# When the second layer's adaLN vectors are made, how many tiles of the halved half-steps stay plain, and the sizes of the feed-forward pieces

## The chip, the core and the metric

The kernel runs on one core of a Trainium2 chip. The metric is the device time of one execution in microseconds. Before the change it is 2717.73 us, the median of three runs (2717.67 to 2719.18). The engines are TensorE (PE in the rows, PEld its weight loads), VectorE (DVE), ScalarE (ACT), GpSimd (POOL) and SyncE (SP); the last two only issue transfers here.

## What is computed

A diffusion trunk of two layers over 512 latent and 256 context tokens of width 1024, in fp32. Both streams use the same weights; the adaLN vectors (shift, scale and gate) differ. Per layer:

```python
x += 1/2 * gate1 * SwiGLU_a(mod1(RMSNorm(x)))   # first half-step, d_ff = 2816
h  = mod2(RMSNorm(x)); p = h @ W_in             # mixer: pool | retention q,k,v,g | conv
x += gate2 * concat[pool, retention, conv] @ W_out
x += 1/2 * gate3 * SwiGLU_b(mod3(RMSNorm(x)))   # second half-step
# mod(h) = h * (1 + scale) + shift;  SwiGLU(h) = (silu(h @ w1) * (h @ w3)) @ w2
# 9 vectors per layer and stream: silu(c) @ w_mod;   at the end RMSNorm of the latent stream
```

## The kernel before

Every fp32 product is three matmuls of the faster fp32r type (lines 164 to 166): each operand is split into a high part (a cast, ScalarE, line 159) and a low part (a subtraction, VectorE, line 160). So every weight block (128x1024, `raw`, then `wh` and `wl`) costs ScalarE and VectorE about a microsecond each, and every product's result does too. Weights are loaded by SyncE in the order of `weight_order`; four split blocks stand ready at most.

The stages follow one another: half-step (0,0) by `ffn`, mixer 0, half-step (0,1) by `ffn_halved`, half-step (1,0) by `ffn_halved`, mixer 1, half-step (1,1) by `ffn`, which has only the latent stream left, in two halves. A half-step has 22 tiles of 128 hidden channels. `ffn` takes them in pieces (PIECES): for every tile the products `up` of w1 and w3 for the context (256 columns) and the latents (512 columns), then `silu` and the product `g`, and after the piece the products `down` into 8 output tiles, added to x. In the last piece the context's `down` come first, then the latents'; each group's squares are summed (`acc`), and `norm_steps` makes the next norm: `ms` (a matmul that sums the squares), a chain of small VectorE operations, `diag`, `rstd` (a matmul that spreads the result), then `ht` and `h`.

`ffn_halved` works in pairs of tiles. It saves matmuls with a scheme of seven products instead of eight (`up_halved`: 7 products of 4 k-tiles, 3 matmuls of 384 columns each, for two weight halves and two column halves of h). This needs sums and differences of the weights (VectorE, lines 601 to 609) and of h: `differences` makes four sets, one per k-tile, each of 8 VectorE operations, 3 casts on ScalarE and 3 subtractions on VectorE. The first pair of tiles is plain, as in `ffn`, and the differences are made meanwhile. x is not in SBUF in these stages: `add_kept` scales a `down` result on ScalarE (`xpart`, line 229), and a transfer from GpSimd's queue adds it to `xkept` in HBM (line 231); only the last pair loads x again.

The adaLN vectors of a layer are nine chunks (l, j). A chunk (`mod_chunks`) is 8 loads of 512 KB (`wm`, two buffers, SyncE's queue), 32 multiply-additions on VectorE (`macc`, lines 319 and 321), 4 turns and 4 folds (`mturn`, `mrow`, lines 329 and 330), one matmul `mods` (line 337) and 8 additions (line 346). It is a generator that runs as a task beside the main program: `spawn(task, delay)` lets it begin after so many microseconds of TensorE work planned so far, each `yield` names the wait to its next step, `poll` runs what is due, and `drain` runs all that is left at once. A scheduler then sets the order of each engine from dependences and the order in which the program was written. Before the change the chunks (0,3) to (0,8) and (1,0) to (1,2) run beside (0,0), (1,3) and (1,4) beside (0,1), (1,5) to (1,8) beside (1,0). Chunk (0,2) is a task of its own, drained after the `up` products of the first piece of (0,0).

Of the kernel before, what the change touches and what calls it, by code (L numbers as in the profile page):

```python
# [15 lines left out]
P = 128  # L16
# [4 lines left out]
DEPTH = 2  # L21
DFF = 2816
NF = DFF // P
PIECES = (4, 4, 4, 4, 4, 2)
MAXP = max(PIECES)
HEADS = 4
WINDOWS = (2, 4, 8, 16)
# [8 lines left out]
NFIRST = 2  # L36
# [1 line left out]


HALVED = ((0, 1), (1, 0))  # L40
HK, HN, SUB = KD // 2, NT // 2, 2
PARKED = ((0, 1), (1, 1), (0, 2), (1, 0))


# [37 lines left out]
class Kernel:  # L82
# [436 lines left out]
    def weight_order(self):  # L519

        ins = self.ins

        def halved(l, s):
            f0 = 0
            for npc in PIECES:
                w2 = ins["w2"][l, s, :, f0 * D : (f0 + npc) * D].rearrange("p (d f n) -> p d f n", d=KD, f=npc)
                for a in range(0, npc, SUB):
                    for f in range(f0 + a, f0 + a + SUB):
                        both = [ins["w13"][l, s, f, :, m * 1024 : (m + 1) * 1024] for m in range(2)]
                        if f < NFIRST:  # L530
                            yield from both
                        else:
                            yield both
                    for d in range(0, KD, 4):
                        yield w2[:, d : d + 4, a : a + SUB]
                f0 += npc

        def ffn(l, s):
            f0 = 0
            for npc in PIECES:  # L540
                for f in range(f0, f0 + npc):
                    for m in range(2):
                        yield ins["w13"][l, s, f, :, m * 1024 : (m + 1) * 1024]
                n = npc * P * per_block(npc)
                for c in range(f0 * D, (f0 + npc) * D, n):
                    yield ins["w2"][l, s, :, c : c + n]
                f0 += npc

        for l in range(DEPTH):
            yield from (halved if (l, 0) in HALVED else ffn)(l, 0)  # L550
            for i in range(4, 8) if l < DEPTH - 1 else range(4):
                yield ins["w_feat"][l, i]
            for i in range(4) if l < DEPTH - 1 else range(4, 8):
                yield ins["w_feat"][l, i]
            for i in range(4):
                yield ins["w_tok"][l, i]
            for i in (10, 11, 12, 13, 8, 9, 14, 15, 16, 17):
                yield ins["w_feat"][l, i]
            for i in range(2):
                for dt2 in range(KD // 2):  # L560
                    yield ins["w_out"][l, i, dt2]
            yield from (halved if (l, 1) in HALVED else ffn)(l, 1)

    def fetch(self, src):
        raws = []
        for a in src if isinstance(src, list) else [src]:
            n = a.shape[-1] if len(a.shape) == 2 else 1024
            raws.append(self.raw(n))
            to = raws[-1] if len(a.shape) == 2 else raws[-1].rearrange("p (d f n) -> p d f n", d=4, f=SUB)
            self.nc.sync.dma_start(to, a)  # L570
        return raws

# [145 lines left out]
    def differences(self, h, T):  # L718

        nc = self.nc  # L720
        for kt in range(HK):
            b11, b12, b21, b22 = self.sums(h, kt)
            nc.vector.tensor_sub(b11, b12, b11)
            nc.vector.tensor_sub(b12, b22, b12)
            nc.vector.tensor_sub(b22, b22, b11)
            nc.vector.tensor_sub(b21, b21, b22)
            for i, t in ((3, b12), (2, b22), (4, b21)):
                for p in range(2):
                    T[i][p][kt] = self.slot("t", F32R)[:, :HN]
                self.split(t, T[i][0][kt], T[i][1][kt])  # L730
            yield 3.6

    def first_difference(self, h):
        nc = self.nc
# [64 lines left out]
    def ffn_halved(self, l, s, h, starts, grps, ends, done):  # L799
# [1 line left out]
        idx = 2 * s  # L801
        accs = {}
        T = {i: [[None] * HK for _ in range(2)] for i in (2, 3, 4)}
        for f0 in range(0, NF, SUB):
            g = self.empty()
            last = f0 == NF - SUB

            def load():
                for st in (CTX, LAT):
                    self.load_x(st, self.kept[st])  # L810

            if f0 == 0:
                ws = {f: self.w13() for f in range(SUB)}
                for grp in starts:
                    self.need(grp)
                    if grp is starts[-1]:
                        task = self.spawn(self.differences(h, T), 1.0)
                    self.up(ws, range(SUB), h, g, grp)
                self.drain(task)
                self.first_difference(h)  # L820
            else:
                for f in range(SUB):
                    self.up_halved(f, h, T, g, load if last and f == SUB - 1 else None)
            w2 = []

            def down(dt, grp, ps, fs):
                self.products([(ps, w2[dt // 4], dt % 4 * SUB * P + fs[0] * P)], g, grp, fs, fs[0] == 0, fs[-1] == SUB - 1)

            if last:
                w2 = [self.weights() for _ in range(2)]  # L830
                for grp in ends:
                    for dt in range(KD):
                        ps = self.psum("down")[:, : grp[2]]
                        down(dt, grp, ps, range(SUB))
                        xd = self.xs(dt, grp)
                        nc.vector.scalar_tensor_tensor(xd, ps, self.gate(l, idx, grp[0], dt), xd, op0=ALU.mult, op1=ALU.add)  # L836
                        self.square(dt, grp, accs)
                    done(grp, accs)
            else:
                for d in range(0, KD, 2):  # L840
                    if d % 4 == 0:
                        w2.append(self.weights())
                    these = [(dt, grp, self.psum("down")[:, : grp[2]]) for dt in (d, d + 1) for grp in grps]
                    for fs in ((0,), (1,)):
                        for dt, grp, ps in these:
                            down(dt, grp, ps, fs)
                    for dt, grp, ps in these:
                        self.add_kept(dt, grp, ps, self.gate(l, idx, grp[0], dt))


    def project(self, w, h, grp, s):
# [444 lines left out]
    def run(self):  # L1296
# [59 lines left out]
            self.up(w0, [1], h, g, G_CTX)  # L1356

        self.first = [self.spawn(self.mod_chunks([(0, 2)], 4.0), 10.0)]
        later = self.spawn(self.mod_chunks([(0, j) for j in range(3, 9)] + [(1, j) for j in range(3)], 6.0), 80.0)
        for l in range(DEPTH):  # L1360
            last = l == DEPTH - 1
            grps = (G_LAT,) if last else both
# [9 lines left out]
                self.drain(later)  # L1372
                self.decays()
            else:
                later = self.spawn(self.mod_chunks([(l, j) for j in range(5, 9)], 11.2), 20.0)
                self.ffn_halved(l, 0, h, both, both, both, done)
                self.drain(later)

# [1 line left out]
            self.mixer(l, h1, grps, cuts, done)  # L1380

            if not last:
                later = self.spawn(self.mod_chunks([(l + 1, j) for j in range(3, 5)], 6.84), 40.0)
                h, done = next_norm(l + 1, 0)
            else:
                done = self.final
# [136 lines left out]
```

## Time and profile before

| | before |
|---|---|
| median of 3 runs | 2717.73 us |
| the profiled execution | 2717.79 us, its span 2715.9 us |
| TensorE busy | 2533.0 us, 93% |
| VectorE, ScalarE, GpSimd busy | 68%, 39%, 11% |
| granted TensorE clock, mean | 0.966 |

The profile comes from one execution. Its span runs from the first to the last instruction; 1.9 us of the time lie around it. A busy TensorE is not one at its peak, since matmuls are pipelined; so the distance from one matmul's start to the next, the share of its weight loads and the granted clock are read beside the busy time. In a row of a timeline the brackets at the end hold the time in which the engine stood idle just before, and what ended it.

### The profile page before, as it was taken

What the parts mean: (1) busy time and instruction counts of PE and PEld (TensorE: products, weight loads), DVE (VectorE), ACT (ScalarE), POOL (GpSimd) and SP (SyncE); (2) the same over time, 40 slices, a digit from 0 to 9 for tenths busy, and PEclk for the clock granted to TensorE, in tenths of its full rate; (3) what the DMA queues carried; (4) which work ended last, traced back from release to release, by engine and by line L of the source; (5) the groups of instructions that cost most, each with busy time, mean ns of one, the idle gap of its engine ahead of it and who ended that gap; (6) DMA issues with size and microseconds to landing.
All of it is one profiled execution on the core that took longest, in us unless ns stands there. A gap on an engine that the chain in (4) does not pass through costs nothing.

```text
span 2715.9 us, 36761 instructions
## 1 busy us (share of the span) xinstructions
PE 2533.0 (93%) x13906; PEld 2247.8 (83%) x13906; DVE 1835.3 (68%) x3430; ACT 1050.3 (39%) x1840; POOL 304.4 (11%) x348
## 2 busy tenths in 40 slices
PE   8999999980999997999999869999998999999997
PEld 4888888870888887899999759999998888888886
DVE  6957767779597688775454787776776696643434
ACT  3221221221134544545555445555554245422222
POOL 0000000000000202323323022424240001000000
PEclk9999999995999998999999989999999999999998
DMA  7533433342132535775757446878675234322221
GB/s 260 166 106 124 143 129 124 116 156 103 39 89 80 112 119 134 174 183 122 155 118 156 148 90 174 184 173 177 165 155 189 86 99 104 105 94 101 93 93 40
DMA packets 156946, 351.67 MB, mean 129 GB/s; under 512 B 16224, under 2 KB 60768, under 8 KB 156768
## 3 DMA queue, kind: packets, MB, share of 16 engines
q1 hardware_dynamic: 104160, 276.94, 30.1%
q0 software_dynamic: 49536, 68.18, 16.0%
q10 hardware_dynamic: 3072, 4.20, 0.6%
q8 instruction: 109, 1.79, 0.3%
q14 instruction: 69, 0.57, 0.1%
HBM read 263.27 MB, written 81.79 MB: 127 GB/s over the span
## 4 chain that ended last, share of the span: by engine, by line
PE 44%; issue 8%; DVE 3%; DMA 1%; ACT 1%; POOL 0%; ACTq 0%; DVEq 0%; POOLq 0%; SPq 0%
PE up L164 9%; PE up L165 9%; PE up L166 9%; PE down L164 5%; PE down L165 5%; PE down L166 5%; DVE acc L419 1%; DVE wl L160 0%; DMA xkept<-xpart 0%; DMA x<-xkept 0%; DVE x L836 0%; DVE macc L321 0%; PE ms L427 0%; PE rstd L443 0%; ACT wh L159 0%
## 5 line engine op out<-in xcount | busy, mean ns | idle before, releaser
L160 DVE TENSOR_TENSOR wl<-raw,wh 128x1024 fp32r<-128x1024 f32 (+1 forms) x408 | 470.9, 1158 | 405.8 <-ACT wh L159 393.8
L159 ACT CAST wh<-raw 128x1024 fp32r<-128x1024 f32 (+1 forms) x408 | 407.1, 1001 | 864.4 <-PE up L165 325.3
L164 PE MATMUL up<-h,wh 128*128 128x512 f32 (+2 forms) x1856 | 636.2, 345 | 4.3 <-ACT h L506 3.9
L165 PE MATMUL up<-h,wh 128*128 128x512 f32 (+2 forms) x1856 | 637.7, 344 | 0.5 <-DVE h L508 0.3
L166 PE MATMUL up<-h,wl 128*128 128x512 f32 (+2 forms) x1856 | 636.3, 344 | 0.1
L231 POOL DMA_DIRECT2D xkept<-xpart x344 | 304.2, 1420 | 1995.4 <-ACT xpart L229 1957.7
L164 PE MATMUL down<-g,wh 128*128 128x256 f32 (+1 forms) x1248 | 427.7, 351 | 51.5 <-ACT g L159 47.0
L165 PE MATMUL down<-g,wh 128*128 128x256 f32 (+1 forms) x1248 | 433.2, 348 | 0.0
L166 PE MATMUL down<-g,wl 128*128 128x256 f32 (+1 forms) x1248 | 429.4, 346 | 0.0
L164 PEld LDWEIGHTS up<-h,wh 128*128 128x128 f32 x1856 | 350.5, 189 | 36.9 <-ACT h L506 5.9
L165 PEld LDWEIGHTS up<-h,wh 128*128 128x128 f32 x1856 | 351.3, 189 | 31.6 <-DVE h L508 1.8
L166 PEld LDWEIGHTS up<-h,wl 128*128 128x128 f32 x1856 | 351.2, 189 | 29.1 <-DVE wl L160 0.3
L321 DVE SCALAR_TENSOR_TENSOR macc<-wm,sc,macc 128x512 f32<-128x512 f32 x462 | 321.3, 744 | 22.3 <-DMA wm<-in_w_mod_dram 22.0
L164 PEld LDWEIGHTS down<-g,wh 128*128 128x128 f32 x1248 | 236.5, 192 | 87.3 <-ACT g L159 53.9
L166 PEld LDWEIGHTS down<-g,wl 128*128 128x128 f32 x1248 | 239.5, 192 | 30.1 <-DVE wl L160 0.2
L165 PEld LDWEIGHTS down<-g,wh 128*128 128x128 f32 x1248 | 240.1, 193 | 29.3 <-DVE g L160 1.9
L229 ACT ACTIVATE xpart<-down,gate 128x256 f32<-128x256 f32 x320 | 173.3, 583 | 88.3 <-PE down L166 87.3
L164 PE MATMUL up<-t,wh 128*128 128x384 f32 x480 | 160.6, 335 | 2.8 <-ACT half L765 2.8
L166 PE MATMUL up<-t,wl 128*128 128x384 f32 x480 | 160.4, 334 | 0.0
L165 PE MATMUL up<-t,wh 128*128 128x384 f32 x480 | 160.4, 334 | 0.0
L691 DVE SCALAR_TENSOR_TENSOR x<-down,gate,x 128x512 f32<-128x512 f32 (+1 forms) x152 | 95.8, 634 | 74.6 <-PE down L166 74.2
L654 DVE TENSOR_TENSOR silu<-silu,up 128x256 f32<-128x256 f32 (+1 forms) x76 | 43.9, 578 | 133.2 <-PE up L166 133.2
(210 smaller groups left out, 3365.5 us busy)
## 6 DMA issues: line engine op xcount, KB each, us to landing
raw<-in_w_dram SPq DMA_DIRECT2D x260, 512.0 KB, 3.7
wm<-in_w_mod_dram SPq DMA_DIRECT2D x128, 512.0 KB, 3.6
xkept<-xpart POOLq DMA_DIRECT2D x176, 256.0 KB, 8.5
xkept<-xpart POOLq DMA_DIRECT2D x168, 128.0 KB, 8.0
raw<-in_w_feat_dram SPq DMA_DIRECT2D x36, 512.0 KB, 3.6
xkept<-x SPq DMA_DIRECT2D x44, 256.0 KB, 2.4
x<-xkept SPq DMA_DIRECT2D x44, 256.0 KB, 6.3
wm<-in_w_mod_dram SPq DMA_DIRECT2D x32, 256.0 KB, 5.8
```

The source lines that it names most:

```text
L159: self.nc.scalar.copy(hi, src)
L160: self.nc.vector.tensor_sub(lo, src, hi.bitcast(F32))
L164: nc.tensor.matmul(out, wh, xh, start=start, stop=False, skip_group_check=shared)
L165: nc.tensor.matmul(out, wh, xl, start=False, stop=False, skip_group_check=shared)
L166: nc.tensor.matmul(out, wl, xh, start=False, stop=stop, skip_group_check=shared)
L229: self.nc.scalar.activation(part, ps, AF.Copy, scale=gate)
L231: self.nc.gpsimd.dma_start(self.kept[st][:, c0 : c0 + n], part, accum_op=ALU.add)
L321: self.nc.vector.scalar_tensor_tensor(acc[v], raw, s, acc[v], op0=ALU.mult, op1=ALU.add)
L419: nc.vector.tensor_add(accs[grp], accs[grp], sq)
L654: nc.vector.tensor_mul(t, t, ps[f, 1])
L691: nc.vector.scalar_tensor_tensor(xd, ps, self.gate(l, idx, grp[0], dt), xd, op0=ALU.mult, op1=ALU.add)
```

## The change

Three things change. The pieces are 2, 4, 4, 4, 4, 4 tiles instead of 4, 4, 4, 4, 4, 2: so the drain of chunk (0,2) stands after two tiles, and the last piece has four. In `ffn_halved` the first four tiles are plain, in two pairs; the four sets of differences are released over these, with waits of 22, 7 and 10 us between them, and are drained after the second pair; the last group has four halved tiles, so its w2 blocks hold 2 output tiles by 4 tiles. And the chunks (1,0) to (1,2) leave half-step (0,0): five chunks run beside (0,1), from 110 us at a pace of 8.0 (before: two, from 40 at 6.84); the four beside (1,0) start at 110 us with a pace of 9.5 (before: 20 and 11.2).

```diff
-PIECES = (4, 4, 4, 4, 4, 2)
+PIECES = (2, 4, 4, 4, 4, 4)
...
-HK, HN, SUB = KD // 2, NT // 2, 2
+HK, HN, SUB, WHOLE = KD // 2, NT // 2, 2, 4
...
-                for a in range(0, npc, SUB):
-                    for f in range(f0 + a, f0 + a + SUB):
+                sub = npc if f0 + npc == NF else SUB
+                for a in range(0, npc, sub):
+                    for f in range(f0 + a, f0 + a + sub):
                         both = [ins["w13"][l, s, f, :, m * 1024 : (m + 1) * 1024] for m in range(2)]
-                        if f < NFIRST:
+                        if f < WHOLE:
                             yield from both
                         else:
                             yield both
-                    for d in range(0, KD, 4):
-                        yield w2[:, d : d + 4, a : a + SUB]
+                    per = 8 // sub
+                    for d in range(0, KD, per):
+                        yield w2[:, d : d + per, a : a + sub]
...
-            yield 3.6
+            yield (22.0, 7.0, 10.0, 0.0)[kt]
...
-        for f0 in range(0, NF, SUB):
+        f0 = 0
+        while f0 < NF:
             g = self.empty()
-            last = f0 == NF - SUB
+            n = SUB if f0 < NF - PIECES[-1] else PIECES[-1]
+            last = f0 + n == NF
+            per = 8 // n
...
-            if f0 == 0:
-                ws = {f: self.w13() for f in range(SUB)}
-                for grp in starts:
+            if f0 < WHOLE:
+                ws = {f: self.w13() for f in range(n)}
+                for grp in starts if f0 == 0 else grps:
                     self.need(grp)
-                    if grp is starts[-1]:
+                    if f0 == 0 and grp is starts[-1]:
                         task = self.spawn(self.differences(h, T), 1.0)
-                    self.up(ws, range(SUB), h, g, grp)
-                self.drain(task)
-                self.first_difference(h)
+                    self.up(ws, range(n), h, g, grp)
+                if f0 + n == WHOLE:
+                    self.drain(task)
+                    self.first_difference(h)
             else:
-                for f in range(SUB):
-                    self.up_halved(f, h, T, g, load if last and f == SUB - 1 else None)
+                for f in range(n):
+                    self.up_halved(f, h, T, g, load if last and f == n - 1 else None)
...
-        later = self.spawn(self.mod_chunks([(0, j) for j in range(3, 9)] + [(1, j) for j in range(3)], 6.0), 80.0)
+        later = self.spawn(self.mod_chunks([(0, j) for j in range(3, 9)], 6.0), 80.0)
...
-                later = self.spawn(self.mod_chunks([(l, j) for j in range(5, 9)], 11.2), 20.0)
+                later = self.spawn(self.mod_chunks([(l, j) for j in range(5, 9)], 9.5), 110.0)
...
-                later = self.spawn(self.mod_chunks([(l + 1, j) for j in range(3, 5)], 6.84), 40.0)
+                later = self.spawn(self.mod_chunks([(l + 1, j) for j in range(5)], 8.0), 110.0)
```

How the order of the engines moves is shown at three places. A row is a line of the kernel, the operation, and what it writes and reads; the numbers in names only tell buffers apart. Lines of the changed kernel are two higher from `differences` on.

On TensorE in the first piece of half-step (0,0), before: `up` products of the piece's fourth tile, then `mods` of chunk (0,2), then the first `down`.

```order
L164 MATMUL up_945<-h_138_523,wh_715 128x512
L165 MATMUL up_945<-h_139_524,wh_715 128x512
L166 MATMUL up_945<-h_138_523,wl_716 128x512
L337 MATMUL mods_1007<-mrow_618,cs 128x64
L164 MATMUL down_1024<-g_145_571,wh_721 128x256
L165 MATMUL down_1024<-g_146_572,wh_721 128x256
```

The same place after the change: `up_647` is the last product of the second tile.

```order
L164 MATMUL up_647<-h_138_523,wh_352 128x256
L165 MATMUL up_647<-h_139_524,wh_352 128x256
L166 MATMUL up_647<-h_138_523,wl_353 128x256
L337 MATMUL mods_757<-mrow_618,cs 128x64
L164 MATMUL down_774<-g_145_571,wh_358 128x256
L165 MATMUL down_774<-g_146_572,wh_358 128x256
```

`mods` and the `down` products have moved ahead of the third and fourth tile, 192 `up` matmuls earlier.

On TensorE at the end of half-step (0,0), before: the last latent `down`, the latent norm's `ms` and `rstd`, the `mods` of the two drained chunks, then the first products of mixer 0 (`cv`, on the context).

```order
L164 MATMUL down_5323<-g_737_5029,wh_5035 128x512
L165 MATMUL down_5323<-g_738_5030,wh_5035 128x512
L166 MATMUL down_5323<-g_737_5029,wl_5036 128x512
L427 MATMUL ms_5334<-ones,acc_5152 128x128 x4
L443 MATMUL rstd_5362<-diag_5351,ones 128x512
L337 MATMUL mods_5449<-mrow_5172,cs 128x64
L337 MATMUL mods_5525<-mrow_5460,cs 128x64
L164 MATMUL cv_5605<-h_788_5246,wh_5041 128x256
```

After the change the latent `ms` stands among the context's `cv` products.

```order
L165 MATMUL cv_5312<-h_770_5116,wh_4880 128x256
L427 MATMUL ms_5340<-ones,acc_5063 128x128 x4
L166 MATMUL cv_5312<-h_769_5115,wl_4881 128x256
L164 MATMUL cv_5313<-h_769_5115,wh_4886 128x256
L165 MATMUL cv_5313<-h_770_5116,wh_4886 128x256
```

No `mods` stands here any more, and the latent `rstd` follows 34 `cv` matmuls later, again with `cv` products behind it.

On VectorE at the start of half-step (0,1), before: the last of four sets of differences (`half`, `t`), then the latent `silu` and `g` of the first pair.

```order
L725 TENSOR_TENSOR half_8869<-half_8869,half_8863 128x384
L160 TENSOR_TENSOR t_8876<-half_8865,t_8875 128x384
L726 TENSOR_TENSOR half_8867<-half_8867,half_8869 128x384
L160 TENSOR_TENSOR t_8880<-half_8869,t_8879 128x384
L160 TENSOR_TENSOR t_8884<-half_8867,t_8883 128x384
L654 TENSOR_TENSOR silu_8899<-silu_8899,up_8704 128x512
L160 TENSOR_TENSOR g_1400_8903<-silu_8899,g_1399_8902 128x512
```

After: the end of the first set, the splits of weights, `silu` and `g`, and then the second set (line 717).

```order
L160 TENSOR_TENSOR t_8506<-half_8489,t_8505 128x384
L160 TENSOR_TENSOR wl_8277<-raw_8274,wh_8276 128x1024
L160 TENSOR_TENSOR wl_8283<-raw_8280,wh_8282 128x1024
L160 TENSOR_TENSOR wl_8289<-raw_8286,wh_8288 128x1024
L656 TENSOR_TENSOR silu_8593<-silu_8593,up_8470 128x512
L160 TENSOR_TENSOR wl_8610<-raw_8607,wh_8609 128x1024
L160 TENSOR_TENSOR g_1313_8597<-silu_8593,g_1312_8596 128x512
L656 TENSOR_TENSOR silu_8600<-silu_8600,up_8472 128x512
L160 TENSOR_TENSOR g_1316_8604<-silu_8600,g_1315_8603 128x512
L717 TENSOR_TENSOR half_8641<-h_1232_8128,h_1233_8129 128x384
```

Three of the four sets have moved behind `silu` and `g`. The start of (1,0) moves in the same way. At the end of (0,1) TensorE has `ms`, `rstd` and `mods` of chunk (1,4) in a row after the last `down`, and then the context's `up` of the next stage; before, those `up` products stood around `ms` and `rstd`, and no `mods` there.

## Rows read from the trace of the kernel before

**Rows 1.** The page, part 1: engine, busy us, share of the span, instructions

```profile
PE 2533.0 (93%) x13906; PEld 2247.8 (83%) x13906; DVE 1835.3 (68%) x3430; ACT 1050.3 (39%) x1840; POOL 304.4 (11%) x348
```

**Rows 2.** Waits of TensorE, whole span: us in total, times, longest us

```profile
PE mods L337 <- DVE mrow L330: 53.9, 2, 27.4
PE down L164 <- ACT g L159: 47.0, 7, 21.9
PE ms L427 <- DVE acc L419: 24.0, 8, 8.8
PE rstd L443 <- DVE diag L434: 21.9, 6, 8.8
```

**Rows 3.** Windows: length, each engine's busy us (instructions), granted clock, DMA share, GB/s

```profile
78.60:111.90 33.30, 33.30 (x194) 29.52 (x193) 31.02 (x49) 7.64 (x12) 0.00 (x0) 1.00 0.60 199
...
590.00:682.60 92.60, 17.09 (x56) 12.22 (x57) 86.42 (x180) 16.93 (x28) 0.00 (x0) 0.57 0.37 125
...
1015.90:1033.60 17.70, 0.17 (x3) 0.01 (x1) 16.87 (x32) 5.62 (x12) 0.00 (x0) 0.60 0.16 60
...
1068.00:1200.00 132.00, 123.95 (x697) 115.84 (x696) 102.60 (x167) 66.87 (x118) 37.65 (x44) 0.99 0.71 175
1200.00:1500.00 300.00, 300.00 (x1718) 285.20 (x1717) 150.11 (x227) 163.13 (x284) 89.67 (x102) 1.00 0.67 142
1500.00:1548.00 48.00, 41.46 (x256) 37.96 (x255) 37.63 (x89) 20.58 (x37) 0.00 (x0) 0.96 0.51 184
1576.00:1598.10 22.10, 0.18 (x2) 0.08 (x1) 22.10 (x41) 5.57 (x11) 0.00 (x0) 0.57 0.26 95
...
1637.00:2063.00 426.00, 426.00 (x2450) 405.36 (x2449) 303.29 (x495) 232.27 (x404) 127.50 (x144) 1.00 0.74 174
2063.00:2103.00 40.00, 33.48 (x205) 29.53 (x203) 32.70 (x83) 15.92 (x31) 0.00 (x0) 0.96 0.44 156
2664.00:2702.00 38.00, 32.40 (x184) 28.78 (x184) 19.19 (x51) 13.71 (x32) 0.00 (x0) 0.96 0.00 1
```

**Rows 4.** Windows of 6 us behind the stalls of (0,1) and (1,0)

```profile
1033.50:1039.50 6.00, 5.91 (x16) 4.70 (x17) 5.24 (x11) 1.68 (x4) 0.00 (x0) 0.50 0.00 0
...
1598.00:1604.00 6.00, 5.98 (x19) 4.89 (x20) 6.00 (x11) 1.41 (x3) 0.00 (x0) 0.58 0.30 94
```

**Rows 5.** Timeline of TensorE in the full stretch: start us, us, what

```profile
579.79 0.39 PE L166 MATMUL up<-h,wl 128*128 128x512 f32 x1
580.02 0.39 PE L164 MATMUL up<-h,wh 128*128 128x512 f32 x1
...
580.70 0.28 PE L164 MATMUL down<-g,wh 128*128 128x256 f32 x1
```

**Rows 6.** Timeline of TensorE: `mods` in the first piece and at the end of (0,0)

```profile
111.90 0.33 PE L337 MATMUL mods<-mrow,cs 128*128 128x64 f32 x2
...
654.09 0.69 PE L337 MATMUL mods<-mrow,cs 128*128 128x64 f32 x2 [26.54 <-DVE mrow L330]
...
682.16 0.69 PE L337 MATMUL mods<-mrow,cs 128*128 128x64 f32 x2 [27.38 <-DVE mrow L330]
```

**Rows 7.** VectorE from 78.6 to 110.2 by line: busy us, mean ns, idle before

```profile
L321 DVE SCALAR_TENSOR_TENSOR macc<-wm,sc,macc 128x512 f32<-128x512 f32 x26 | 17.6, 743 | 0.0
...
L329 DVE STREAM_TRANSPOSE mturn<-macc 128x512 f32<-128x512 f32 x4 | 2.7, 694 | 0.0
L330 DVE TENSOR_REDUCE mrow<-mturn 128x16 f32<-128x512 f32 x4 | 2.6, 676 | 0.0
L160 DVE TENSOR_TENSOR g<-silu,g 128x256 fp32r<-128x256 f32 (+1 forms) x5 | 2.6, 517 | 0.5 <-ACT g L159 0.5
L654 DVE TENSOR_TENSOR silu<-silu,up 128x256 f32<-128x256 f32 (+1 forms) x4 | 1.9, 476 | 0.0
L319 DVE TENSOR_SCALAR macc<-wm,sc 128x512 f32<-128x512 f32 x2 | 0.9, 477 | 0.0
```

**Rows 8.** Waits of TensorE from 1068 to 1200: us in total, times, longest us

```profile
PE down L164 <- ACT g L159: 5.3, 3, 4.1
```

More of the change, by code (lines that the diff above doesn't have):

```diff
@@ L568, in fetch @@
             raws.append(self.raw(n))
-            to = raws[-1] if len(a.shape) == 2 else raws[-1].rearrange("p (d f n) -> p d f n", d=4, f=SUB)
+            to = raws[-1] if len(a.shape) == 2 else raws[-1].rearrange("p (d f n) -> p d f n", d=a.shape[1], f=a.shape[2])
             self.nc.sync.dma_start(to, a)
@@ L810, in load @@
                     self.load_x(st, self.kept[st])
-            if f0 == 0:
-                ws = {f: self.w13() for f in range(SUB)}
-                for grp in starts:
+            if f0 < WHOLE:
+                ws = {f: self.w13() for f in range(n)}
+                for grp in starts if f0 == 0 else grps:
                     self.need(grp)
-                    if grp is starts[-1]:
+                    if f0 == 0 and grp is starts[-1]:
                         task = self.spawn(self.differences(h, T), 1.0)
-                    self.up(ws, range(SUB), h, g, grp)
-                self.drain(task)
-                self.first_difference(h)
-            else:
-                for f in range(SUB):
-                    self.up_halved(f, h, T, g, load if last and f == SUB - 1 else None)
+                    self.up(ws, range(n), h, g, grp)
+                if f0 + n == WHOLE:
+                    self.drain(task)
+                    self.first_difference(h)
+            else:
+                for f in range(n):
+                    self.up_halved(f, h, T, g, load if last and f == n - 1 else None)
             w2 = []
             def down(dt, grp, ps, fs):
-                self.products([(ps, w2[dt // 4], dt % 4 * SUB * P + fs[0] * P)], g, grp, fs, fs[0] == 0, fs[-1] == SUB - 1)
+                self.products([(ps, w2[dt // per], dt % per * n * P + fs[0] * P)], g, grp, fs, fs[0] == 0, fs[-1] == n - 1)
             if last:
-                w2 = [self.weights() for _ in range(2)]
+                w2 = [self.weights() for _ in range(KD // per)]
                 for grp in ends:
@@ L833, in ffn_halved @@
                         ps = self.psum("down")[:, : grp[2]]
-                        down(dt, grp, ps, range(SUB))
+                        down(dt, grp, ps, range(n))
                         xd = self.xs(dt, grp)
@@ L840, in ffn_halved @@
                 for d in range(0, KD, 2):
-                    if d % 4 == 0:
+                    if d % per == 0:
                         w2.append(self.weights())
@@ L848, in ffn_halved @@
                         self.add_kept(dt, grp, ps, self.gate(l, idx, grp[0], dt))
+            f0 += n
     def project(self, w, h, grp, s):
```

## The prediction

> **What bounds the kernel now.** I read the page first: TensorE is busy 93% of the span and no other engine over 68% [rows 1], so time is won only where TensorE stands still, runs at its lower clock, or gets less to do. Next the waits of TensorE over the span: three sorts are long, the adaLN matmul `mods` behind VectorE's fold `mrow`, the `down` products behind `g`, and the norm's `ms` and `rstd` behind `acc` and `diag` [rows 2]. Then the span stretch by stretch, to see where they lie [rows 3]. At the end of ffn(0,0), from 590.0 to 682.6, TensorE works 17.09 of 92.60 us; at the start of the two halved stages it works 0.17 of 17.70 and 0.18 of 22.10 us; in the middle of those stages it is full. Around each stall I looked at the granted clock: in the 6 us after the stall of stage (0,1) it is 0.50, after that of (1,0) 0.58, that is the lower of its two levels (1.2 of 2.4 GHz) for some 6 and 5 us, a loss of 3.0 and 2.5 us [rows 4]. Last the single instructions at the two folds [rows 6] and what VectorE does in the first piece [rows 7].
>
> The sum is made against the profiled execution, 2717.8 us (span 2715.9 and 1.9 around it); the median of the runs, 2717.73, is the same to 0.1.
>
> **The change part by part.**
>
> *A, the first piece has 2 tiles instead of 4.* The drain of chunk (0,2) now stands behind tile 1. TensorE reaches that place at 78.60. There the order before went on with the third and fourth tile, and `mods` came at 111.90 with nothing to wait for, while VectorE was busy 31.02 of 33.30 us [rows 3, 6]. Of the chunk VectorE still has to do 26 additions, 2 first products, 4 turns and 4 folds: 17.6 + 0.9 + 2.7 + 2.6 = 23.8 us [rows 7]. With 1.0 us for the `silu` and `g` of the product just ended (476 and 517 ns), `mods` comes near 103.4, so TensorE stands 24.8 us, and then loses 3.0 at the lower clock [rows 4]. A = +28. Bounds: 24 (the chunk alone, no clock loss) and 34 (all that VectorE did in that stretch, 31.0, plus 3). Nothing gives this back: the two tiles are done later at the same price.
>
> *B, the end of ffn(0,0).* Idle there are 92.60 less 17.09, 75.5 us: the longest waits of `rstd` and of `ms`, 8.8 each, the folds of two chunks that nine chunks at this pace left over, 26.54 and 27.38, and 4.0 for the second `rstd` [rows 2, 3, 6]. The granted clock of 0.57 over that stretch [rows 3] takes 17.09 x 0.43 = 7.3 more, and some 3 behind it, as in the stalls of the other stages: 85.8 in all. Now only six chunks run there, and by the order none is left at the end. The last piece has 4 tiles, so that the eight latent `down` products, of 12 matmuls each instead of 6, cover the context norm, and the `cv` products of the context stand on both sides of the latent `ms` and ahead of its `rstd`. Left over I take 5.8, half a wait of `ms` and some clock: B = -80. Bounds: -85 (nothing left) and -72 (one wait of `rstd`, 8.8, with its lower clock, 3, and 2 of `ms`).
>
> *C and G, the starts of (0,1) and (1,0).* Before, all four differences of h stand ahead of the latent `silu` and `g` on VectorE; it is busy 16.87 of the 17.70 us in which TensorE waits, and all of the 22.10 in (1,0), where a mod chunk runs into it too [rows 3]. Now one difference stands there, about a quarter, and the rest lies beside the second pair of plain tiles; the first chunk starts at 110 instead of 40 and 20. Stall and clock cost 17.7 + 3.0 = 20.7 and 21.9 + 2.5 + 1.8 (a short wait after it) = 26.2. I leave about 2 in each: C = -19, G = -24. Bounds: 0 left, or a quarter of the stall and a clock loss (-13 and -18).
>
> *D, five chunks in (0,1) instead of two.* A chunk is eight pieces of 4 additions, each released after the pace, so 8 x 8.0 + 11.7 = 75.7 us of TensorE's planned work apiece now, against 66.4 in (0,1) and 101.3 in (1,0) before. In 1068 to 1200, with chunks at 66.4, TensorE idles 8.05 us, and its weight loads fill 115.84 of 132 us, 87.8%, against 95.1% in 1200 to 1500 without chunks: by that 9.7 us are lost, 4.85 per chunk. In 1637 to 2063, with chunks at 101.3, they fill 95.2%: nothing is lost [rows 3]. VectorE's share of these stretches is 0.78, 0.50 and 0.71. At 75.7 a straight line between the two chunk times gives 4.85 x 25.6 / 34.9 = 3.6 per chunk. But 4.1 of the 8.05 us are one wait of a `down` for `g` soon after the start's stall, which goes [rows 8]; without it the line gives 2.0, and since the loss is still nil at 101.3 it should set in past that, below the line: I take 1.4 per chunk, 7 for five: D = 7 - 9.7 = -3. Bounds: -10 (as at 101.3) and +14.5 (as at 66.4, 24.2 - 9.7).
> The Trainium skill (Perfetto Trace Analysis, Identifying the Most-Contended Engine) says that the busy time of matmuls is no measure of how near TensorE is to its limit, because they are pipelined, and that the busy share of LDWEIGHTS is. By the matmuls alone the two chunks cost 8.05 and the upper bound of D would be +12 instead of +14.5; the trace agrees with the skill in so far as the share of weight loads shows 1.7 us that the busy time hides, and it clears the full 426.00 of 426.00 us of that doubt.
>
> *E, four plain tiles instead of two, in two stages.* A plain tile is 48 matmuls of 512 columns and 48 of 256, 36864 columns; a halved one 84 of 384, 32256. 512 columns take 580.02 - 579.79 = 0.23, four of them to 580.70 0.91, so 0.2275 [rows 5]. 4608 columns more are 2.05 us, four tiles 8.2: E = +8.2. Against it, ten rounds of kept sums become nine, with 16 accumulating transfers fewer on POOL's queue per stage; POOL is busy under a third of these stretches, so that counts nothing.
>
> *F, the end of (0,1).* Before, the context `up` products of the next stage covered the latent norm; 48.00 - 41.46 = 6.5 us idle and 1 to 2 for the clock [rows 3]. Now the last fold of chunk (1,4) falls into that norm on VectorE, and on TensorE `ms`, `rstd` and `mods` stand in a row ahead of the context `up`: one uncovered wait of `rstd` (8.8 [rows 2]). F = +9; bounds +3 (the wait replaces those there) and +16 (also `ms` at 8.8, less what was there).
>
> *H, pace 9.5 instead of 11.2 in (1,0)*: 87.7 us per chunk, near the 101.3 that cost nothing: +1 (0 to 5). *I, the end of (1,0)*: of 6.5 us idle in 2063 to 2103 [rows 3], 4-tile `down` products twice as long cover the norm's waits: -5 (-6.5 to 0). *J, the end of (1,1)*: 5.6 us idle in 2664 to 2702 [rows 3], I read this as `down` products of two tiles that end before VectorE has squared and added what came before them; with four tiles each takes twice as long, also ahead of the last norm: -7 (-10 to -4).
>
> Sum: 28 - 80 - 19 - 3 + 8.2 + 9 - 24 + 1 - 5 - 7 = -91.8, so 2626 us.
>
> **The rivals.**
> 1. *The chunks cost in (0,1) what they cost before*: D = +14.5 instead of -3, 2643.5. For it: only 12% lies between the two paces. Against it: half of the idle time was that one wait. Chance 0.2.
> 2. *The stall of the starts only moves*: three differences now stand among the weight splits of the second pair, and TensorE could wait for those splits or for the second `g`. Then C and G are lost: 2626 + 43 = 2669. For it: VectorE has the same work at that place. Against it: the second pair gives TensorE 2 x 36864 columns, 33 us, of `up` products that don't need the differences. Chance 0.1.
> 3. *VectorE can't carry five chunks in (0,1)*, the other side: a chunk that nothing hides takes 682.16 - 654.09 = 28.1 us [rows 6]; five take 140, D = +130.7, 2760. It ends slower than before once 98.5 of the 140, 70%, are open. Against it: VectorE at 0.78 of a stretch lost TensorE 9.7 us for two chunks, 17%. Chance 0.05, of which 0.02 end near that point.
> 4. *Less is repaired at the end of ffn(0,0)*: the order covers the norms only if VectorE keeps up there, and 0.93 of that stretch it is busy; with a wait of `ms` and one of `rstd` left, 17.6, and their clock, B is -65 and the time 2641. Chance 0.07.
>
> **How the numbers follow.** The forecast has 0.58. Its bounds, as the root of their summed squares, reach 12 below the sum and 24 above it, 2614 to 2650, and hold rivals 1 and 4. The left values (what remains of a stall) are chosen rather than measured, so I double the lower reach and add a quarter to the upper one: 2602 to 2656. Outside lie rivals 2 and 3, 0.15. About 0.2% (5 us) is what a measurement of this kernel can tell from no change: slower has 0.03 and same 0.02, both of rival 3; all the rest, 0.95, is faster.
>
> **What would show it.** In the profile of the changed kernel: a wait of about 25 us of `mods` behind `mrow` near 80 to 104 and the lower clock behind it (A); no wait over 5 us between 590 and 640 (B); no wait of a `down` for `g` over 5 us (C, G); weight loads at or above 93% of the stretch with chunks in (0,1) (D; 88% is rival 1); a wait of `rstd` of some 9 us at that stage's end (F). The prediction is wrong if `mods` in the first piece comes early or is hidden, if the wait for `g` is still there, or if VectorE is full between the starts and ends of (0,1).

## The result

The changed kernel takes 2647.53 us, the median of four runs (2645.30 to 2650.29), against 2718.43 (2717.67 to 2719.18) in the same comparison: a ratio of 0.974, 95% interval 0.9723 to 0.9757. That is 71 us faster; 92 were forecast. The profiled execution took 2645.30 us (span 2643.5), 72.5 less than that of before; it is the lowest of the four.

The waits of TensorE over the span of the changed kernel, longest sorts first (us in total, times, longest us); they answer to [rows 2]:

```profile
PE mods L337 <- DVE mrow L330: 23.0, 1, 23.0
PE ms L427 <- DVE acc L419: 17.5, 6, 6.4
PE down L164 <- ACT g L159: 16.2, 7, 3.4
PE up L164 <- ACT half L767: 10.3, 6, 6.4
...
PE rstd L443 <- DVE diag L434: 8.5, 4, 3.1
PE down L164 <- ACT xpart L229: 7.0, 4, 1.7
```

The two folds of 26.5 and 27.4 us and the stalls of 17.5 and 21.9 us behind `g` are gone; a new wait for `mrow`, of 23.0, is there, and two sorts are longer than before: `up` behind `half`, 10.3 us in six waits, and `down` behind `xpart`, 7.0 in four.

To see which place gained what, the span is cut at the same instructions in both traces. The columns are those of [rows 3]: length of the stretch, then each engine's busy time. Before: the end of (0,0) up to the mixer's first latent product; in stage (0,1) the first pair from its latent `up` on, the second pair, the middle, the end; in (1,0) the first pair, the second, and the rest up to a product of mixer 1.

```profile
580.70:696.67 115.97, 40.09 (x216) 34.58 (x214) 99.48 (x232) 24.83 (x43) 0.00 (x0) 0.63 0.34 115
993.25:1052.75 59.50, 41.97 (x194) 34.96 (x193) 54.27 (x98) 27.53 (x50) 10.27 (x12) 0.83 0.21 45
1052.75:1104.87 52.12, 48.02 (x265) 45.08 (x264) 40.41 (x63) 25.29 (x45) 13.52 (x16) 0.97 0.73 182
1104.87:1506.43 401.56, 397.60 (x2274) 377.63 (x2273) 228.36 (x353) 215.27 (x374) 117.62 (x133) 1.00 0.70 156
1506.43:1551.40 44.97, 36.80 (x222) 31.83 (x221) 36.28 (x89) 18.46 (x35) 0.00 (x0) 0.93 0.40 147
1551.40:1618.56 67.16, 43.49 (x193) 35.94 (x194) 61.88 (x110) 28.28 (x51) 8.23 (x10) 0.79 0.22 55
1618.56:1664.69 46.13, 46.13 (x265) 43.82 (x264) 35.19 (x54) 25.18 (x45) 15.67 (x18) 1.00 0.76 181
1664.69:2130.43 465.74, 457.51 (x2594) 429.78 (x2593) 322.03 (x554) 241.25 (x426) 117.75 (x133) 0.99 0.68 165
```

The same places in the changed kernel, ahead of them the wait in the first piece:

```profile
78.03:101.06 23.03, 0.00 (x1) 0.01 (x1) 21.72 (x36) 0.94 (x2) 0.00 (x0) 0.61 0.63 197
589.82:637.39 47.57, 47.57 (x305) 43.16 (x304) 38.68 (x104) 21.26 (x37) 0.00 (x0) 1.00 0.37 125
933.95:979.32 45.37, 40.85 (x194) 34.06 (x193) 35.83 (x63) 23.15 (x42) 8.26 (x10) 0.96 0.30 77
979.32:1037.48 58.16, 52.60 (x289) 45.58 (x288) 27.53 (x46) 21.33 (x39) 14.17 (x18) 0.97 0.42 76
1037.48:1429.36 391.88, 382.98 (x2181) 366.23 (x2180) 304.23 (x498) 204.41 (x356) 105.28 (x119) 0.99 0.74 181
1429.36:1500.11 70.75, 55.59 (x319) 48.63 (x319) 62.49 (x138) 25.43 (x45) 0.00 (x0) 0.90 0.50 167
1500.11:1545.46 45.35, 40.83 (x194) 34.03 (x193) 26.95 (x50) 19.08 (x35) 8.01 (x9) 0.96 0.30 75
1545.46:1603.85 58.39, 53.26 (x289) 46.18 (x288) 28.29 (x47) 21.33 (x39) 14.38 (x17) 0.94 0.42 77
1603.85:2064.65 460.80, 455.72 (x2594) 430.06 (x2592) 342.94 (x590) 233.10 (x410) 104.83 (x119) 0.99 0.67 168
```

Up to the first latent product of mixer 0 the change gains 696.67 - 637.39 = 59.3 us. Stage (0,1) gives back 8.0: it takes 1500.11 - 933.95 = 566.2 instead of 1551.40 - 993.25 = 558.2. Stage (1,0) gains 14.5 (564.5 instead of 579.0), and the rest 6.6. So the first half of the forecast was exceeded, and the halved stages, which were to gain 33 together (C to I of the forecast), gained 6.5.

### The profile page after: what moved, and what is told of

Read it like the earlier page. It is cut to its first block, busy times and chain, and to the rows that moved or that the text cites. A ratio compares the mean times of both kernels' runs of the same rounds, so it can differ in the third digit from the quotient of the medians.

```text
span 2643.5 us, 36683 instructions
## 1 busy us (share of the span) xinstructions
PE 2536.2 (96%) x14002; PEld 2250.5 (85%) x14002; DVE 1808.0 (68%) x3390; ACT 1017.6 (38%) x1780; POOL 276.3 (10%) x316
## 5 line engine op out<-in xcount | busy, mean ns | idle before, releaser
L159 ACT CAST wh<-raw 128x1024 fp32r<-128x1024 f32 (+1 forms) x400 | 399.9, 1004 | 894.7 <-PE up L165 362.4
L160 DVE TENSOR_TENSOR wl<-raw,wh 128x1024 fp32r<-128x1024 f32 (+1 forms) x400 | 462.7, 1162 | 357.8 <-ACT wh L159 348.5
L164 PE MATMUL up<-h,wh 128*128 128x512 f32 (+2 forms) x1920 | 659.9, 345 | 9.2 <-ACT half L767 6.7
L165 PE MATMUL up<-h,wh 128*128 128x512 f32 (+2 forms) x1920 | 659.8, 344 | 0.2
L166 PE MATMUL up<-h,wl 128*128 128x512 f32 (+2 forms) x1920 | 658.6, 344 | 0.0
L231 POOL DMA_DIRECT2D xkept<-xpart x312 | 276.1, 1378 | 1957.7 <-ACT xpart L229 1914.3
L164 PEld LDWEIGHTS up<-h,wh 128*128 128x128 f32 x1920 | 363.8, 190 | 43.7 <-ACT half L767 8.2
L165 PEld LDWEIGHTS up<-h,wh 128*128 128x128 f32 x1920 | 364.7, 190 | 32.7 <-DVE h L508 0.7
L166 PEld LDWEIGHTS up<-h,wl 128*128 128x128 f32 x1920 | 364.2, 190 | 31.5
L164 PEld LDWEIGHTS down<-g,wh 128*128 128x128 f32 x1264 | 239.5, 193 | 55.7 <-ACT g L159 18.7
L229 ACT ACTIVATE xpart<-down,gate 128x256 f32<-128x256 f32 (+1 forms) x288 | 154.4, 586 | 68.1 <-PE down L166 62.0
L164 PE MATMUL up<-t,wh 128*128 128x384 f32 x432 | 145.3, 336 | 3.7 <-ACT half L767 3.7
L166 PE MATMUL up<-t,wl 128*128 128x384 f32 x432 | 144.9, 335 | 0.0
L165 PE MATMUL up<-t,wh 128*128 128x384 f32 x432 | 144.7, 335 | 0.0
```

Of the source, the lines that this page charges most:

```text
L159: self.nc.scalar.copy(hi, src)
L160: self.nc.vector.tensor_sub(lo, src, hi.bitcast(F32))
L164: nc.tensor.matmul(out, wh, xh, start=start, stop=False, skip_group_check=shared)
L165: nc.tensor.matmul(out, wh, xl, start=False, stop=False, skip_group_check=shared)
L166: nc.tensor.matmul(out, wl, xh, start=False, stop=stop, skip_group_check=shared)
L229: self.nc.scalar.activation(part, ps, AF.Copy, scale=gate)
```

## The experiments

All ratios are against runs of the kernel before in the same comparison, three rounds each.

**The three parts, each alone on the kernel before.** The moved chunks:

```
-        later = self.spawn(self.mod_chunks([(0, j) for j in range(3, 9)] + [(1, j) for j in range(3)], 6.0), 80.0)
+        later = self.spawn(self.mod_chunks([(0, j) for j in range(3, 9)], 6.0), 80.0)
...
-                later = self.spawn(self.mod_chunks([(l, j) for j in range(5, 9)], 11.2), 20.0)
+                later = self.spawn(self.mod_chunks([(l, j) for j in range(5, 9)], 9.5), 110.0)
...
-                later = self.spawn(self.mod_chunks([(l + 1, j) for j in range(3, 5)], 6.84), 40.0)
+                later = self.spawn(self.mod_chunks([(l + 1, j) for j in range(5)], 8.0), 110.0)
```

> The kernel before with the third part of the change alone: six chunks beside (0,0), five beside (0,1) from 110 us at pace 8.0, four beside (1,0) from 110 at 9.5; pieces and plain tiles as before. Theory: the two folds at the end of (0,0) go (53.9 us and the lower clock, some 60 together), the start of (1,0) loses a mod chunk's work among its differences (-8), the end of (0,1) pays the drained chunk (+9 to +20), the chunks in (0,1) cost no more than two did (+0 to +3): about -45, 2673. Rival (VectorE or the loads can't carry five chunks beside (0,1) when only two tiles are plain): waits inside 1100 to 1500 sum to over 20 us and the time stays above 2690.

Measured: 2649.15 us, ratio 0.9752 (0.9736 to 0.9767), 70 us faster: this part alone is worth what the whole change is. More than the folds went. Waits of TensorE at the end of (0,0), before and then with this part:

```profile
PE mods L337 <- DVE mrow L330: 53.9, 2, 27.4
PE rstd L443 <- DVE diag L434: 12.8, 2, 8.8
PE ms L427 <- DVE acc L419: 9.2, 2, 8.8
```

```profile
PE rstd L443 <- DVE diag L434: 4.3, 2, 2.8
...
PE ms L427 <- DVE acc L419: 0.3, 1, 0.3
```

The norm's waits fall from 22.0 to 4.6 us, although the last piece still has two tiles. Most of them came from the same chunks, whose work stood among the norm's on VectorE: their multiply-additions (line 321) fill 10.1 us there from 590.0 to 627.6 in the kernel before, and none from 580 to 640 with this part. The forecast had given that gain to the four-tile piece.

The plain tiles and the spread differences alone (the change's diff without PIECES and without the three `spawn` lines):

> The kernel before with the second part alone: four plain tiles in the halved stages and the differences of h spread over them; pieces and chunks as before. Theory (a plain pair has its own price of 7 to 8 us at its end, beside 4.1 us of matmuls): the starts lose 15 us each instead of 21.1 and 28.7, and the stages have 8.2 us more matmuls, so the time falls by 11 us only, to about 2707. Rival (the forecast: what the differences cost goes, and a pair costs only its matmuls): -35, 2683.

Measured: 2710.91 us, ratio 0.9976 (0.9966 to 0.9986), 8 us faster, where the forecast's price gives 35 for the two starts. The chunks still start at 40 and 20 us in this run, and a wait of 3.6 us of `up` for `xpart` comes in between the two pairs of (0,1); but the waits for `g` that the theory names, of 2.8 and 3.4 us, are there without the other two parts. The price of a pair by its columns alone is refuted.

The pieces alone:

```
-PIECES = (4, 4, 4, 4, 4, 2)
+PIECES = (2, 4, 4, 4, 4, 4)
```

> The kernel before with the first part alone: pieces of 2, 4, 4, 4, 4, 4 tiles; chunks and plain tiles as before. If the parts add, the change's 71 us less 70 of the chunks and 8 of the plain tiles leave +6, 2725: the wait of mods in the first piece (+26) against what the four-tile last piece gives at the ends of (0,0) and (1,1). Rival: the last piece of four gives at the end of (0,0) what the forecast put there (norm waits of 8.8 and 8.8 covered): then +26 - 17 - 6 = +3 or less, and faster than before if one of the folds gets covered as well.

Measured: 2719.47 us, ratio 1.0006 (0.9996 to 1.0015), no change. The 23.1 us in the first piece are there; at the end of (0,0) the waits sum to 57.2 instead of 75.9, because one fold is half covered:

```profile
PE mods L337 <- DVE mrow L330: 40.8, 2, 27.3
PE ms L427 <- DVE acc L419: 13.1, 1, 13.1
PE rstd L443 <- DVE diag L434: 3.3, 1, 3.3
```

The three parts alone sum to some 75 us, against 71 together; the intervals don't tell these apart. In the traces the pieces alone take 18.7 us of waits from the end of (0,0), a gain that the moved chunks bring for the most part already: with them alone some 7 us of waits are left there.

**The first piece.** The changed kernel with

```
-PIECES = (2, 4, 4, 4, 4, 4)
+PIECES = (4, 2, 4, 4, 4, 4)
```

> The changed kernel with pieces of 4, 2, 4, 4, 4, 4 tiles: the drain of chunk (0,2) stands behind four tiles again, and the last piece still has four. Theory: the wait of mods for mrow in the first piece (23.0 us in the changed kernel) and the lower clock behind it (3.1) are lost time and nothing later gives them back, so the time falls by 25 us, from 2647.5 to about 2622, and no wait of mods over 1 us is left. Rival: the stall only moves, because VectorE is behind by the chunk's work wherever it stands, or because a piece of two tiles waits in second place: then a wait of 10 us or more appears between 100 and 200 us and the time stays above 2637.

Measured: 2618.10 us (2611.58 to 2622.40), ratio 0.9633 (0.9614 to 0.9652), 29 below the changed kernel, where 25 were expected; the four runs lie 10.8 us apart. Its list of waits of TensorE is empty from 60 to 650 us. The stall was lost time, and it doesn't move.

**What a plain pair costs.** In the changed kernel TensorE still waits for `g` at the end of both plain pairs. This is ScalarE at the end of the first (columns: start us, us, what, in brackets the idle time before), then VectorE and TensorE:

```profile
947.95 0.52 ACT L159 CAST t<-half 128x384 fp32r<-128x384 f32 x1 [0.59 <-DVE half L728]
953.69 2.95 ACT L159 CAST wh<-raw 128x1024 fp32r<-128x1024 f32 x3 [5.23 <-PE up L165]
956.55 0.58 ACT L655 ACTIVATE silu<-up 128x512 f32<-128x512 f32 x1
957.04 1.03 ACT L159 CAST wh<-raw 128x1024 fp32r<-128x1024 f32 x1
958.91 0.62 ACT L159 CAST g<-silu 128x512 fp32r<-128x512 f32 x1 [0.84 <-DVE silu L656]
```

```profile
954.78 3.50 DVE L160 TENSOR_TENSOR wl<-raw,wh 128x1024 fp32r<-128x1024 f32 x3 [5.73 <-ACT wh L159]
958.19 0.68 DVE L656 TENSOR_TENSOR silu<-silu,up 128x512 f32<-128x512 f32 x1
...
959.58 0.50 PE L164 MATMUL down<-g,wh 128*128 128x512 f32 x1 [2.78 <-ACT g L159]
```

ScalarE's part of the differences (`t`) is done by 948.5. It then stands idle for 5.23 us until TensorE's latent `up` frees a weight buffer: the pair's four blocks hold all four. The next three splits come at once, 2.95 us on ScalarE and 3.50 on VectorE, on both ahead of `silu`, and the cast of `g` ends at 959.5; TensorE has been waiting since 956.80 [2.78 us]. Three experiments test this. Without the sets of differences, in the changed kernel (e2) and in the one before (e3):

```
-            b11, b12, b21, b22 = self.sums(h, kt)
-            nc.vector.tensor_sub(b11, b12, b11)
...
-                self.split(t, T[i][0][kt], T[i][1][kt])
+            for i in (3, 2, 4):
+                for p in range(2):
+                    T[i][p][kt] = h[p][kt][:, :HN]
```

> The changed kernel without the four sets of differences of h in both halved stages: their VectorE and ScalarE instructions are left out, and the products read h in their place. The changed kernel loses 15 us at the start of each halved stage, at the ends of its two plain pairs (waits of down for g of 2.8 and 3.4 us, of down for xpart of 1.7 each, and slower matmuls behind them). Theory: this is a plain pair's own price, since the pair holds all four buffers of split weights until its latent products end, and the splits of the next blocks then stand ahead of silu and g; without the sets those waits stay within 1 us and the time falls by less than 6 us, to 2642 to 2647. Rival: the sets are still in the way of g, only less: the waits fall below 1 us and the time falls by 15 to 30 us, to 2618 to 2632.

Measured: 2640.62 us, ratio 0.9716 (0.97 to 0.9733), 7 us below the changed kernel, just past the bound. Waits of TensorE from 950 to 1035, with the sets and then without:

```profile
PE down L164 <- ACT g L159: 6.2, 2, 3.4
PE down L164 <- ACT xpart L229: 3.5, 2, 1.7
```

```profile
PE down L164 <- ACT g L159: 6.2, 2, 3.4
PE down L164 <- ACT xpart L229: 1.7, 1, 1.7
```

The waits for `g` are the same, and the stage (1,0) shows the same numbers in both kernels. Of these waits the sets cause one for `xpart` per stage, 3.5 us of the 7 in both; the rest of the 7 was not traced to a place.

> The kernel before without the four sets of differences of h in both halved stages: their instructions are left out and the products read h in their place. Theory: at the start of each halved stage only the plain pair's own price is left, some 7 us of the 21.1 and 28.7 us lost there (in (1,0) a mod chunk's work besides), so the time falls by about 14 + 14 to 14 + 21, to 2684 to 2690, and waits of down for g of 2 to 8 us remain at both places. Rival: the whole stall is the sets': no wait over 1 us remains and the time falls by 45 or more, below 2674.

Measured: 2688.89 us, ratio 0.9897 (0.9882 to 0.9912), 28 us faster, as the theory has it. Of the stall of 17.5 us a wait remains that the sets don't make, as long as at the second pair of the changed kernel:

```profile
1018.83 0.79 PE L164 MATMUL down<-g,wh 128*128 128x512 f32 x1 [3.38 <-ACT g L159]
```

The second pair tile by tile, in the changed kernel:

```
+                    for f in range(n):
+                        ws = {f: self.w13()}
+                        for grp in grps:
+                            self.up(ws, [f], h, g, grp)
```

> The changed kernel with the second plain pair of each halved stage made tile by tile, context and latents of one tile before the next, as the plain half-steps do it; so two of the four weight buffers come free after the first of the two tiles. Theory (a pair's own price comes from holding four buffers and ending both tiles at once): the waits at the end of the second pair, 3.4 and 1.7 us and some slower matmuls, 8 us per stage, fall to 3 or less, and the time falls by 8 to 14 us, to about 2636. Rival: the price comes from the sets or from ScalarE's xpart alone: the waits stay and the time moves by less than 4 us.

Measured: 2635.15 us, ratio 0.9701 (0.9686 to 0.9715), 12 us below the changed kernel. From 950 to 1035 the wait of 3.38 is gone and that of the first pair stays:

```profile
PE down L164 <- ACT xpart L229: 3.5, 2, 1.7
PE down L164 <- ACT g L159: 2.8, 1, 2.8
```

**The end of (0,1).** The changed kernel with the five chunks from 60 us:

```
-                later = self.spawn(self.mod_chunks([(l + 1, j) for j in range(5)], 8.0), 110.0)
+                later = self.spawn(self.mod_chunks([(l + 1, j) for j in range(5)], 8.0), 60.0)
```

> The changed kernel with the five chunks beside half-step (0,1) starting at 60 us instead of 110, so that the last of them, (1,4), is folded before the stage ends and the context's up products of the next stage stand around the latent norm again. Theory: the end of (0,1), 22.1 us lost in the changed kernel, returns to the 13 of the kernel before, and the time falls by 6 to 10 us, to about 2639. Rival: the earlier chunks run into the differences and plain pairs at the start, which then lose as much: the time stays within 4 us, with waits of down for g of 6 us or more near 1000.

Measured: 2627.59 us, ratio 0.9672 (0.9657 to 0.9686), 20 us below the changed kernel: twice the upper end of the theory. The end of the stage is then full, where the changed kernel idled 70.75 - 55.59 = 15.2 us at a clock of 0.90:

```profile
1400.00:1480.00 80.00, 79.97 (x490) 75.36 (x489) 62.73 (x137) 35.20 (x62) 0.00 (x0) 1.00 0.52 178
```

Before, with a last group of two and no drained chunk, TensorE idled 44.97 - 36.80 = 8.2 us here. So the last group of four can cover the norm, and the drained chunk had hidden that gain besides its own price; no run parts the two.

**The middle of (0,1).** There the changed kernel has one long wait, 6.42 us, and slower matmuls behind it. TensorE at that place, ScalarE, VectorE, and SyncE's issues:

```profile
1242.37 0.69 PE L164 MATMUL up<-h,wh 128*128 128x384 f32 x1 [6.42 <-ACT half L767]
```

```profile
1241.43 0.52 ACT L782 ACTIVATE half<-half 128x384 f32<-128x384 f32 x1 [8.73 <-DVE half L781]
1241.86 0.46 ACT L767 COPY half<-up 128x384 f32<-128x384 f32 x1
```

```profile
1229.43 2.74 DVE L321 SCALAR_TENSOR_TENSOR macc<-wm,sc,macc 128x512 f32<-128x512 f32 x4 [3.80 <-DMA wm<-in_w_mod_dram]
...
1238.26 0.75 DVE L321 SCALAR_TENSOR_TENSOR macc<-wm,sc,macc 128x512 f32<-128x512 f32 x1 [5.93 <-DMA wm<-in_w_mod_dram]
...
1240.84 0.56 DVE L781 TENSOR_TENSOR half<-up,half 128x384 f32<-128x384 f32 x1
```

```profile
1225.66 6.87 SPq L373 DMA_DIRECT2D wm<-in_w_mod_dram  x2
```

VectorE isn't busy: it stands before a multiply-addition whose load hasn't landed (issued at 1225.66, it takes 12.5 us), with a `half` queued behind it. ScalarE waits 8.73 us for that `half` and has the copy queued behind, for which TensorE waits. The edit leaves out seven of a chunk's eight loads and uses the first block in their place:

```
-                    raw = self.wide("wm").rearrange("p (k n) -> p k n", k=2)
-                    nc.sync.dma_start(raw, self.ins["w_mod"][l, j, half, kk])
+                    if l == 0 or j > 4 or half + kk == 0:
+                        raw = self.wide("wm").rearrange("p (k n) -> p k n", k=2)
+                        nc.sync.dma_start(raw, self.ins["w_mod"][l, j, half, kk])
```

> The changed kernel in which each of the five chunks beside (0,1) loads one block of 512 KB instead of eight and uses it eight times; VectorE's work is the same. In the changed kernel TensorE waits 6.4 us near 1236 and runs slower behind it, 9.2 us in all, while VectorE stands at a multiply-addition whose load takes up to 12.5 us to land beside the kept sums' transfers. Theory: the late load is the cause, VectorE's busy time is not; no wait over 2 us is left between 1050 and 1430, and the time falls by 8 to 12 us, to about 2637. Rival: VectorE's work itself is too much there; the wait stays or moves, and the time changes by less than 4 us.

Measured: 2632.69 us, ratio 0.9687 (0.9673 to 0.9702), 15 us below the changed kernel, more than the 8 to 12 expected (12.4 between the profiled executions). VectorE is as busy as before and TensorE hardly waits any more; 1037 to 1420 in the changed kernel, and in this one:

```profile
1037.00:1420.00 383.00, 374.10 (x2129) 357.24 (x2128) 298.02 (x489) 201.30 (x352) 105.76 (x120) 0.99 0.73 177
```

```profile
1037.00:1420.00 383.00, 382.43 (x2206) 366.81 (x2206) 307.65 (x504) 205.65 (x357) 104.71 (x118) 1.00 0.66 146
```

VectorE at 0.80 of a stretch costs TensorE 0.6 us of idle time; the late loads cost the other 8.3 of the 8.9 in the changed kernel.

**Together.** The changed kernel with the edits of e1, e4 and e8:

> The changed kernel with three edits together: pieces 4, 2, 4, 4, 4, 4; the second plain pair tile by tile; the chunks beside (0,1) from 60 us. If the three places are independent, the gains add: -29 - 12 - 20 = -61, 2586. Rival (they share a cause, VectorE's backlog at the start of (0,1)): less than 50 together, above 2597.

Measured: 2587.86 us, ratio 0.9521 (0.9507 to 0.9535), 60 us below the changed kernel and 131 below the one before. The gains, 29, 12 and 20 alone, add. Last, the same with two plain tiles (`WHOLE = 2`, `yield 3.6`):

> The kernel with three edits together (pieces 4, 2, 4, 4, 4, 4; chunks beside (0,1) from 60 us) but with two plain tiles in the halved stages and the differences set as before. With a pair's own price of 7 to 8 us and 4.1 us of matmuls, two more plain tiles cost some 10 to 12 us per stage and save the part of the stall that the sets make: 13 us in (0,1), 8 in (1,0) where no chunk runs into them any more. Theory: the two nearly cancel, 2582 to 2594 against 2587.9. Rival: the plain tiles are worth what the forecast gave them, 11 to 15 us in each stage, 2610 or more.

Measured: 2599.81 us, ratio 0.957 (0.9556 to 0.9584): between the two. The stall behind `g` is 17.5 us in both stages; I had taken 8.5 for (1,0) from e5. There the context's `up` products stand behind the latent norm, and TensorE reaches the first `down` 36.2 us after `rstd`; here it does so after 25.5, so VectorE has less time for the sets. So with cheaper pairs the two plain tiles more, with the differences spread over them, are worth 12 us over both stages.

## Why the prediction came out as it did

The time lay inside the range and 21.5 us above the forecast, by another way than rival 1, whose 2643.5 is close to it. That the range held owes something to luck: E, the term that failed, has no bounds in it; the upward reach of 24 comes mostly from D's bound, 17.5 above its term, and D came near its forecast. Step by step, forecast and then measured (profiled executions, stretches above):

| term | forecast | measured |
|---|---|---|
| A, first piece | +28 | +26: 23.0 idle, 3.0 for the clock |
| B, end of (0,0) | -80 | -85: 59.3 gained, with A inside |
| C and half of E, start of (0,1) | -15 | -2.1: 45.37 - 59.50, and 58.16 - 46.13 |
| D and F, rest of (0,1) | +6 | +10.1: 391.88 + 70.75, and before 52.12 + 401.56 + 44.97 less a halved pair, 46.13 |
| G and half of E, start of (1,0) | -20 | -9.5: 45.35 - 67.16, and 58.39 - 46.13 |
| H and I, rest of (1,0) | -4 | -4.9 |
| J, with mixer 1 | -7 | -6.6 |

*A* was right in mechanism and size. TensorE waits 23.0 us while VectorE is busy 21.72 of them; the 24.8 had counted 26 additions, and 23 were left. The clock behind it is at its lower level for six microseconds:

```profile
101.10:107.10 6.00, 6.00 (x21) 5.42 (x22) 2.53 (x13) 0.00 (x0) 0.00 (x0) 0.50 0.07 27
```

*B* was right in size, and its second reason carried little: nothing is left idle (47.57 of 47.57), but by e5 and e7 the norm's waits go mostly because the chunks do, 17.4 of 22.0 us without any change of the pieces.

*C, G and E* hold the miss, some 23 us of it. The stall was read rightly: three of four sets leave it, and the first pair gains 14.1 and 21.8. The step that failed is E, "4608 columns more are 2.05 us, four tiles 8.2". A plain pair costs more than its matmuls. The second pair takes 58.16 us in place of a halved pair's 46.13: 12.0 more, of which its columns are 4.1. The other 8 are the waits at its end, for `g`, for `xpart`, and slower matmuls behind them. E took a unit's matmuls for its whole price and gave it no bounds. The price was in the trace of before, but unseen, under the stall of the first pair; e3 uncovers it there. In the same way "about 2 left in each" should have been 7. Rival 2 is not what happened: the waits stay when the sets go (e2).

*D* had the right bounds (its idle time is 8.9 against 8.06 us before, plus a lower clock) and the wrong cause. I argued with VectorE's load between two paces. By e10 that load costs next to nothing (0.6 us of 383); a load that lands late does, and the late ones are those beside the transfers of `add_kept` (last section). D's upper bound and rival 1 rest on the same reading of VectorE's load.

*F* measured +7.0 in idle time and some more in clock (0.90 against 0.93), near its +9. It is not the one wait of `rstd` that was forecast: `ms` waits 6.4 us for `acc`, and `rstd` 3.1. And e8 shows that without the drained chunk the place would have been 20 us better, so the forecast was right for a sum of two things, of which it named one. *H, I and J* came out within 1 us.

*Rivals 1, 3 and 4* did not happen: five chunks are carried, and the end of (0,0) is full.

The Trainium skill's rule on weight loads (Perfetto Trace Analysis, Identifying the Most-Contended Engine) made no difference here: they fill 366.23 of 391.88 us in the middle of (0,1), 93.5% against the 95.1% of [rows 3], which is 6.3 us lost, and the busy time of the matmuls already shows 8.9.

## What to carry to other kernels

Price an added unit of work by a whole one in the trace, from its first instruction to the next unit's first, not by its matmuls; where the only one there stands under another stall, its own price is hidden, and an experiment without that stall is what shows it. When a change has several parts, run each alone: here one part was worth the whole gain, and the other two each held a gain and a loss that nearly cancelled. Work that is drained at a fixed place can be paid there twice, by its own time and by what it keeps others from covering.

## What the hardware showed

A load of 512 KB for a chunk lands in 3.6 us in the median over the kernel before; in the middle of (0,1) of the changed kernel (1037 to 1420) it takes 6.5 in the median and up to 12.5. Of the 35 loads there, 24 were under way beside accumulating transfers of `add_kept` and landed after 7.1 in the median; the 11 others after 3.5, and after 4.3 at most. No run leaves these transfers out, so that they are the cause is read from this division. They move less than the plain transfers but hold the engines longer. From 1195 to 1245 in the changed kernel, packets, MB, and share of the 16 engines' time of GpSimd's queue and of SyncE's:

```profile
q0 software_dynamic: 2304, 3.15, 41.6%
q1 hardware_dynamic: 2093, 4.83, 27.8%
```

The granted clock stood at the lower level (0.50) for six microseconds after 17.5 us of waiting as well as after 23.0, and for some five after 21.9 ([rows 4] for the kernel before); after the 23.0 it was 1.00 from 107.1 to 113.1. Why the four runs of e1 lie 10.8 us apart, and those of c1 within 0.9, stays open.
